# The triangular blocks of an RWKV-7 layer turned by VectorE and merged on chip

## The chip, the cores and the metric

The kernel runs as one launch on one core of a Trainium2 chip. The metric is the device time of that launch in microseconds (us); less is better. TensorE is called PE, VectorE DVE, ScalarE ACT, GpSimd POOL and SyncE SP, as in the profile. SP does nothing but issue DMAs, in order; each other engine also works through its own queue in order.

## What is computed

Two layers of a decoder trunk over 1024 positions of width 1024, in float32. The first layer mixes tokens with RWKV-7, the second with a sparse attention; each is followed by a SwiGLU feed-forward and a layer norm, and every part is scaled and shifted by a vector made from the conditioning `c`. The change lies in the RWKV-7 mixer alone:

```python
def _rwkv7_step(S, inp):
    r_t, w_t, k_t, v_t, a_t, b_t = inp
    sa = jnp.einsum('bhij,bhj->bhi', S, a_t)
    S = S * w_t[:, :, None, :] + sa[..., None] * b_t[:, :, None, :] + v_t[..., None] * k_t[:, :, None, :]
    y = jnp.einsum('bhij,bhj->bhi', S, r_t)
    return S, y
...
xs = h[None] + xx[None] * mu[:, None, None, :]
r, k, v = jnp.einsum('pbtd,pde->pbte', xs[:3], w_rkv)
w = -jax.nn.softplus(-(w0 + jnp.tanh(xw @ w1) @ w2)) - 0.5
a = jax.nn.sigmoid(a0 + (xa @ a1) @ a2)
...
_, y = lax.scan(_rwkv7_step, S0, (tm(rh), tm(decay), tm(kh), tm(vh), tm(-kk), tm(kk * ah)))
```

The kernel does not walk through 1024 steps. It takes 16 chunks of 64 positions; inside a chunk the product of the steps becomes the inverse of a triangular 64x64 matrix for each of the 16 heads. Chunk and head make a *unit*: 256 units, 128 in each half of the sequence.

## The kernel before

Everything is kept feature-major: a tile has 128 partitions (two heads of 64 features: a *feature tile*, `ft`, 8 of them) and 512 positions (a half, `hf`, with 8 chunks). Matmuls of the projections are done as three float32r products of a high and a low part (`mm3`, lines 234 to 236).

**Order in time.** A scheduler lays the program onto the engines when it is built, from dependences, the written order and its own durations; what it decides is fixed, and `order` listings below show it. By the trace the first 976 us go like this. Half 0: the head (modulated and transposed input, `rwkv_head`), then in `rwkv_proj` the low-rank parts (L497), the k projection with `k_rest` for each feature tile (to 204 us), the v projection (to 272), the r projection (to 363), into whose end the head of half 1 is interleaved (L385 on DVE makes the mixed inputs, L437 to L440 on PE multiply them). Half 1: L497 from 380, k to 510, v to 568, r to 625. Then the *core*, `chain_chunk` and `pre_chunk`, which goes through the 16 chunks from 625 to 976 (L954 is the first product of a chunk, L989, L1003, L1016, L1019 its chain), with the output projection of finished quarters (`tail`, L1070) between. The feed-forward and the second layer follow.

**The triangular blocks.** `k_rest` makes on PE the 64x64 products of each unit (L572) and masks them on DVE into `en` (L574), which goes to DRAM as `nsd` (L575). A unit's inverse is made from two 32x32 diagonal blocks and one block below. `tinv_dve` inverts diagonal blocks of 128 units at once, one unit per partition, so a block of rows has to become a row per unit: eight POOL DMAs gather it from `nsd` (L627). One *pass* over 128 blocks is 31 steps of two DVE operations (L634, L636; here called T), and there are two passes for each half. The result is turned by one copy (L641) and goes back to DRAM by POOL (`t1d` L639, `tsd` L642). `tinv_merge` makes the block below for 32 units at a time: POOL loads (L651 to L653), 32x32 products on PE (L659), copies on ACT (L660), again, and a store by POOL (L663). Merges of half 0 lie in the v and r loops of half 1, those of half 1 in the core's chunks 1 to 4. `load_chunk` (L933) loads a chunk's inverses into `ttp` by four DMAs on SP.

**Queues around it.** Spilled r, k, v, a, b and the bonus go out on SP (L519, L521, L617), the weights come in on SP (L215). Tiles named `tmp` are a ring of 7 that ACT, DVE and SP's stores share. The low half of a weight (L122) is made on DVE or POOL in turn.

Of the kernel before, what the change touches and what calls it, by code (L numbers as in the profile page):

```python
# [19 lines left out]
P = 128  # L20
# [23 lines left out]
C_ID, C_CEN, C_M, C_M64, C_RST, C_CS, C_CN, C_BLK, C_E4 = 0, 128, 256, 512, 576, 640, 768, 896, 1024  # L44
C_ALL = 1025


def constants():
# [10 lines left out]
    a[:, C_RST:C_RST + 64] = (t != 0)[None, :]  # L59
    a[:, C_CS:C_CS + P] = np.where(p[None, :] <= p[:, None], 0.0, LOWEST)  # L60
    a[:, C_CN:C_CN + P] = np.where(p[None, :] <= p[:, None], 0.0, NEG)
# [20 lines left out]
def trunk(ctx, tc, a, out):  # L82
# [30 lines left out]
    dma2 = nc.gpsimd.dma_start  # L113
# [28 lines left out]
    csr = cp.tile([P, 8, 32], F32, name="csr")  # L142
# [8 lines left out]
    V.tensor_copy(csr, pt[:, 0:8, None].to_broadcast([P, 8, 32]))  # L151
# [33 lines left out]
    ones = cp.tile([P, 1], F32, name="ones")  # L185
    V.memset(ones, 1.0)
    mhalf = cp.tile([P, 8], F32, name="mhalf")
    V.memset(mhalf, -0.5)
    gne = cp.tile([P, 1], F32, name="gne")
# [61 lines left out]
    def ada_mm(o, st, k0):  # L251
        for i, s_ in enumerate(st):
            k = k0 + i
            q = 32 * (k % 4)
            mm(o[q:q + 32, :], csr[:, k, :], s_, start=k < 4, stop=k >= 4, skip_group_check=True)
# [40 lines left out]
    def ada_v(l, j, stage, tmp):  # L296

        acc = tmp()
        for k2 in range(4):
# [3 lines left out]
            for i in range(2):  # L303
                k = 2 * k2 + i
                if k == 0:
                    V.tensor_scalar(acc, st[:, 0:512], csr[:, 0, 0:1], None, op0=OP.mult)
                else:
                    V.scalar_tensor_tensor(acc, st[:, i * 512:i * 512 + 512], csr[:, k, 0:1], acc, op0=OP.mult, op1=OP.add)
# [47 lines left out]
    nsd = [tc.dram_tile([KT, P, HN], F32, name=f"nsd{h}") for h in range(2)]  # L356
    tsd = [tc.dram_tile([128, 64, 64], F32, name=f"tsd{h}") for h in range(2)]
    t1d = [tc.dram_tile([128, 32, 32], F32, name=f"t1d{h}") for h in range(2)]
# [96 lines left out]
    def rwkv_proj(hf, p1, head, between, betweenv):  # L455
# [16 lines left out]
        rstb = cst[:, None, C_RST:C_RST + 64].to_broadcast([P, 8, 64])  # L472
        rst = tmp("rst", 1)
        V.tensor_copy(rst.rearrange("p (c t) -> p c t", t=64), rstb)
# [72 lines left out]
        em = []  # L547

        def k_rest(ft, em):
# [17 lines left out]
            en = tmp("en", 2)  # L567
# [6 lines left out]
            V.tensor_tensor(v3(en), v3(o), cst[:, None, C_M64:C_M64 + 64].to_broadcast([P, 8, 64]), op=OP.mult)  # L574
            dma(nsd[hf][ft], en)  # L575
# [45 lines left out]
    def tinv_dve(hf, tp):  # L621

        for b in range(2):
            n_ = tp.tile([P, 32, 32], F32, tag="tn", name="tn")
# [1005 lines left out]
```

## Time and profile before

| | us |
|---|---|
| median of 3 runs | 3288.55 |
| lowest and highest | 3287.1, 3292.51 |
| the profiled execution, its time | 3285.99 |
| the profiled execution, its span in the trace | 3284.2 |

The profile is one execution. Each engine's busy time is a share of the span; PE's granted clock is given as a share of 2.4 GHz (1.00, and 0.50 is 1.2 GHz), so a stretch with 0.75 ran half of its time at each level. In the table by stretches a row has the length, the busy time of each engine with the number of records in brackets, the mean granted clock, the mean busy share of the 16 DMA engines, and the rate in GB/s. PE's busy time over the whole span is 93%, DVE's 66%, ACT's 41%, POOL's 33%; these averages hide that single stretches are limited by other engines.

### The profile page before, as it was taken

The numbers are of one execution on the slowest core, as the hardware profiler recorded it, in microseconds if no ns is written. First come the engines' busy times: TensorE is split into PE (matmuls) and PEld (weight loads), VectorE is DVE, ScalarE is ACT, GpSimd is POOL, SyncE is SP. The second block draws the span as 40 slices with busy tenths as digits, with TensorE's granted clock in tenths as the row PEclk, the third lists the DMA queues.
The fourth block names the chain that finished last, engine by engine and source line by source line (L and its number), as shares of the span: only waits on it lengthen the run. The fifth ranks groups of instructions, "written<-read, shape, count | busy, mean of one in ns | idle before, by whom it ended". The sixth has DMA issues, their size and how long they took to land. (4 is left out here: it accounts for less than half of the span.)

```text
span 3284.2 us, 49028 instructions
## 1 busy us (share of the span) xinstructions
PE 3047.2 (93%) x17857; PEld 2401.8 (73%) x17857; DVE 2167.8 (66%) x4255; ACT 1350.7 (41%) x2510; POOL 1090.6 (33%) x946
## 2 busy tenths in 40 slices
PE   6988899889999999999899999988999999899998
PEld 2555367678877788888688776677887777687886
DVE  4577888646776665494245487886697788775345
ACT  3552463234444222332223756656522566452223
POOL 3363257442123411251113213555222432443111
PEclk8989999889999999999999999989999999999999
DMA  6466365788854665382534432153323421353333
GB/s 197 134 188 169 89 195 132 160 164 184 188 140 137 200 196 170 116 269 91 116 103 128 138 96 65 58 163 120 98 92 107 137 64 34 100 164 97 93 100 122
DMA packets 540997, 436.34 MB, mean 133 GB/s; under 512 B 134802, under 2 KB 435346, under 8 KB 540754
## 3 DMA queue, kind: packets, MB, share of 16 engines
q1 hardware_dynamic: 534770, 423.74, 44.9%
q0 software_dynamic: 5984, 9.45, 1.5%
q8 instruction: 141, 2.31, 0.3%
q14 instruction: 102, 0.84, 0.1%
HBM read 378.07 MB, written 54.90 MB: 132 GB/s over the span
## 5 line engine op out<-in xcount | busy, mean ns | idle before, releaser
L205 ACT CAST whi<-wst 128x512 fp32r<-128x512 f32 x886 | 541.0, 619 | 1231.8 <-PE psu L235 541.6
L122 POOL TENSOR_TENSOR wlo<-wst,whi 128x512 fp32r<-128x512 f32 x330 | 460.0, 1394 | 1425.6 <-ACT whi L205 1372.1
L122 DVE TENSOR_TENSOR wlo<-wst,whi 128x512 fp32r<-128x512 f32 (+1 forms) x556 | 472.8, 853 | 518.0 <-ACT whi L205 512.7
L234 PE MATMUL psu<-hin,whi 128*128 128x512 f32 (+1 forms) x1568 | 586.8, 375 | 46.0 <-DVE sl L1168 29.7
L235 PE MATMUL psu<-hin,whi 128*128 128x512 f32 (+1 forms) x1568 | 585.6, 373 | 9.7 <-DVE hin L901 3.3
L236 PE MATMUL psu<-hin,wlo 128*128 128x512 f32 (+1 forms) x1568 | 583.5, 372 | 0.1
L234 PEld LDWEIGHTS psu<-hin,whi 128*128 128x128 f32 x1568 | 300.6, 192 | 101.5 <-DVE sl L1168 33.1
L235 PEld LDWEIGHTS psu<-hin,whi 128*128 128x128 f32 x1568 | 301.6, 192 | 61.4 <-DVE hin L901 6.1
L236 PEld LDWEIGHTS psu<-hin,wlo 128*128 128x128 f32 x1568 | 301.1, 192 | 50.5 <-POOL wlo L122 0.5
L235 PE MATMUL psg<-wlo,hid 128*128 128x512 f32 x528 | 206.4, 391 | 0.0
L234 PE MATMUL psg<-whi,hid 128*128 128x512 f32 x528 | 205.1, 391 | 0.0
L236 PE MATMUL psg<-whi,hid 128*128 128x512 f32 x528 | 205.0, 389 | 0.0
L234 PE MATMUL psg<-xs,whi 128*128 128x512 f32 x384 | 159.2, 425 | 22.5 <-ACT whi L205 11.8
L235 PE MATMUL psg<-xs,whi 128*128 128x512 f32 x384 | 162.2, 422 | 9.6 <-POOL xs L122 5.0
L236 PE MATMUL psg<-xs,wlo 128*128 128x512 f32 x384 | 159.3, 417 | 3.2 <-DVE wlo L122 3.2
L1168 DVE TENSOR_TENSOR sl<-sl,psu 128x512 f32<-128x512 f32 (+1 forms) x98 | 61.8, 630 | 138.0 <-PE psu L236 132.2
L234 PEld LDWEIGHTS psg<-xs,whi 128*128 128x128 f32 x384 | 75.1, 197 | 55.6 <-ACT whi L205 14.6
L234 PEld LDWEIGHTS psg<-whi,hid 128*128 128x128 f32 x528 | 99.2, 188 | 20.9
L236 PEld LDWEIGHTS psg<-whi,hid 128*128 128x128 f32 x528 | 99.1, 188 | 20.8
L235 PEld LDWEIGHTS psg<-wlo,hid 128*128 128x128 f32 x528 | 99.2, 188 | 20.7 <-DVE wlo L122 0.4
L116 ACT ACTIVATE z<-z,mx 128x128 f32<-128x128 f32 (+7 forms) x128 | 99.2, 776 | 31.9 <-DVE mx L1533 31.1
L235 PEld LDWEIGHTS psg<-xs,whi 128*128 128x128 f32 x384 | 75.4, 196 | 41.4 <-POOL xs L122 10.2
(424 smaller groups left out, 6562.3 us busy)
## 6 DMA issues: line engine op xcount, KB each, us to landing
wst<-in_ffn_w_in_dram SPq DMA_DIRECT2D x196, 512.0 KB
wst<-in_ffn_w_out_dram SPq DMA_DIRECT2D x92, 512.0 KB
z<-in_ada_w_dram SPq DMA_DIRECT2D x56, 512.0 KB
wst<-in_rwkv_w_rkv_dram SPq DMA_DIRECT2D x48, 512.0 KB
wst<-in_rwkv_w_out_dram SPq DMA_DIRECT2D x64, 256.0 KB
wst<-in_dsa_w_out_dram SPq DMA_DIRECT2D x32, 512.0 KB
wst<-in_dsa_w_in_dram SPq DMA_DIRECT2D x26, 512.0 KB
wst<-in_ada_w_dram SPq DMA_DIRECT2D x24, 512.0 KB
```

Source lines behind the costliest of these rows:

```text
L116: return A.activation(o, i, f, **kw)
L122: i = eng.tensor_tensor(lo, x, hi.bitcast(F32), op=OP.subtract)
L205: A.copy(h_[:, :m], st[:, c:c + m])
L234: mm(o, lh, rh, start=first, stop=False)
L235: mm(o, lh, rl, start=False, stop=False)
L236: mm(o, ll, rh, start=False, stop=last)
L1168: V.tensor_tensor(sl[:, c], sl[:, c], ou[:, c], op=OP.mult)
```

## The change

The triangular blocks no longer go through DRAM between `k_rest` and the inverse. `k_rest` masks its product into two tiles for every four feature tiles (`nm0`, `nm1`: the columns 0 to 31 and 32 to 63 of each unit; two DVE operations 128x256 in place of one 128x512). After the fourth feature tile a new generator `tinv` is queued: DVE's 32x32 block transposes bring the blocks from rows to units (one of 128x1024 and two of 32x1024), the 31 steps follow as before (they read the turned block in contiguous runs), two more transposes turn the result back, and the merge's products are made straight from these tiles (`nm0`, `xt`, `t1`) with 32 units to a copy. A pass now holds both diagonal blocks of the 64 units of four feature tiles, where it held one block of 128 units. `invert(n)` takes n steps of the passes that are queued: 4 after each feature tile of the v loop, 9 in the r loop, the rest at the end of the half's own `rwkv_proj`. The results go to DRAM on SP as `tdd` and `tod`, and `load_chunk` loads them with six DMAs of 128-byte runs in place of four of 128 and 256 bytes. No DMA of this part is on POOL any more (166 were). Smaller edits: the conditioning `csr` is kept once and broadcast by the matmul's operand, the constants are 833 columns in place of 1025, `rst` is set by memsets, one mask is made from another.

```diff
-        ti = [tinv_dve(hf, tpA) for hf in range(2)]
+        def invert(n):
+            for _ in range(n):
+                while inv and next(inv[0], inv) is inv:
+                    inv.pop(0)
...
         def between0(i):
...
                 take(hg[1], 1)
+                invert(9)
+            if i == 16:
+                invert(100)
...
-        rwkv_proj(0, p1, heads[0], between0, lambda i: take(ti[0], 0))
+        rwkv_proj(0, p1, heads[0], between0, lambda i: invert(4))
...
-            V.tensor_tensor(v3(en), v3(o), cst[:, None, C_M64:C_M64 + 64].to_broadcast([P, 8, 64]), op=OP.mult)
-            dma(nsd[hf][ft], en)
+            for i in range(2):
+                c_ = slice(32 * i, 32 * i + 32)
+                V.tensor_tensor(nm_[i][:, ft % 4], v3(o)[:, :, c_],
+                                cst[:, None, C_M64 + 32 * i:C_M64 + 32 * i + 32].to_broadcast([P, 8, 32]), op=OP.mult)
+            if ft % 4 == 3:
+                inv.append(tinv(hf, ft // 4, *nm_))
...
+        turn = lambda o, i: V.transpose(o, i)
+        turn(n_, fl(n0).rearrange("p u t -> p t u"))
+        for q in (1, 3):
+            turn(n_[qs[q]], fl(n1)[qs[q]].rearrange("p u t -> p t u"))
...
+        xt = tpA.tile([P, 32, 32], F32, tag="tn", name="xt")
+        turn(xt.rearrange("p u t -> p t u"), x_)
+        t1 = tpA.tile([P, 32, 32], F32, tag="tx", name="t1")
+        turn(t1, xt)
+        dma(tdd[hf][:, 4 * g:4 * g + 4].rearrange("p a c t -> p (a c t)"), xt.rearrange("p u t -> p (u t)"))
+        yield
+        for i in range(2):
+            us = range(16 * i, 16 * i + 16)
+            rhs = xt[:, 16 * i:16 * i + 16]
+            for lh, ro in ((fl(n0), 1), (t1, 0)):
+                o = pst()
+                for e in range(2):
+                    k, m = qs[2 * e + ro], qs[2 * e]
+                    for u in us:
+                        v = u - 16 * i
+                        mm(o[m, v * 32:v * 32 + 32], lh[k, u, :], rhs[k, v, :], start=True, stop=True)
+                r_ = inv_tmp[0]()
+                for e in range(2):
+                    A.copy(r_[qs[2 * e]], o[qs[2 * e], :])
+                rhs = r_.rearrange("p (u t) -> p u t", t=32)
+            for e in range(2):
+                dma(tod[hf][e, :, 4 * g + 2 * i:4 * g + 2 * i + 2].rearrange("r a c t -> r (a c t)"), r_[qs[2 * e]])
+            yield
...
             for e in range(2):
-                for r, j in ((0, 0), (32, 32)):
-                    last = dma(tt_[64 * e + r:64 * e + r + 32, :, e, j:],
-                               dap(tsd[hf], (c * 16 + e) * 4096 + r * 64 + j, [[64, 32], [2 * 4096, KT], [1, 64 - j]]))
+                r0 = 64 * e
+                dma(tt_[r0:r0 + 32, :, e, 0:32], tdd[hf][r0:r0 + 32, :, c, :])
+                dma(tt_[r0 + 32:r0 + 64, :, e, 32:64], tdd[hf][r0 + 32:r0 + 64, :, c, :])
+                last = dma(tt_[r0:r0 + 32, :, e, 32:64], tod[hf][e, :, :, c, :])
...
-            if 1 <= gc < 5:
-                tinv_merge(1, gc - 1, pc)
```

Where the work stands on the engines follows from the new written order. Three places matter below. In the listings `tt` and `tx` are the tiles of the inverse's steps, `psg` a projection's PSUM bank, `xs` the mixed input; lines of before and after differ by a few (L381 after is L385 before, L663 after is L659 before, L643 and L645 are the steps L634 and L636).

**First place: DVE at the end of half 0's k loop.** Before, this stretch holds only the work of `k_rest`, the mixing of the v inputs (L385, L126) and low halves of weights; the steps begin some 30 rows further down.

```order
L552 COPY f_111<-d 128x8
L558 TENSOR_TENSOR tmp<-tmp,av 128x512
L385 SCALAR_TENSOR_TENSOR tmp<-h,vf,tmp 128x512
L122 TENSOR_TENSOR xs<-tmp,xs 128x512
L126 TENSOR_SCALAR xs<-tmp 128x512
L574 TENSOR_TENSOR en<-pst,cst 128x512
```

After, the three transposes (L629) that turn the first four feature tiles and the first steps of pass 1 stand among the same work:

```order
L554 TENSOR_TENSOR tmp<-tmp,av 128x512
L629 STREAM_TRANSPOSE tn<-nm_982 128x1024
L119 TENSOR_TENSOR wlo<-wst,whi 128x512
L556 TENSOR_TENSOR sp<-tmp,em 128x512
L629 STREAM_TRANSPOSE tn<-nm_983 32x1024 x2
L552 SCALAR_TENSOR_TENSOR sp<-tmp,d 128x512
L643 TENSOR_TENSOR tt<-tn,tx 128x31
L587 TENSOR_SCALAR tmp<-psu 128x512
```

Pass 1 moved forward into the k loop's end; in half 1 the same happens with pass 3 (rows of the same kind).

**Second place: the seam between half 0 and half 1.** On PE before, the r projection's end (L234 to L236) is interleaved with the head of half 1:

```order
L235 MATMUL psg<-xs,whi 128x512
L236 MATMUL psg<-xs,wlo 128x512
L439 MATMUL psl<-tmp,lr 128x512
L440 MATMUL pst<-tmp,lr_2000 32x512
L437 MATMUL psl<-tmp,lr 64x512
L438 MATMUL psl<-tmp,lr 64x512
L439 MATMUL psl<-tmp,lr 128x512
L440 MATMUL pst<-tmp,lr_2000 32x512
L614 MATMUL psu<-tmp,cst 128x512
```

After, the 128 merge products of pass 2 stand in a row ahead of all of that head (L433 after is L437 before):

```order
L231 MATMUL psg<-xs,whi 128x512
L232 MATMUL psg<-xs,wlo 128x512
L663 MATMUL pst<-xt,nm_1370 32x32 x32
L663 MATMUL pst<-tmp,t_2571 32x32 x32
L663 MATMUL pst<-xt,nm_1370 32x32 x32
L663 MATMUL pst<-tmp,t_2571 32x32 x32
L615 MATMUL psu<-tmp,cst 128x512
L230 MATMUL psg<-xs,whi 128x512
```

On DVE at the same seam the steps of pass 2 were strung out between the head's mixing and half 1's decay (L509, a scan):

```order
L634 TENSOR_TENSOR tt<-tn,tx 128x256
L385 SCALAR_TENSOR_TENSOR sp<-h,vf,sp 128x512
L122 TENSOR_TENSOR xs<-ta,xs 128x512
L126 TENSOR_SCALAR xs<-sp 128x512
L636 TENSOR_TENSOR tx<-tx,tt 128x16x16
L509 SCALAR_TENSOR_TENSOR tmp<-rst,tmp 128x512
L126 TENSOR_SCALAR xs<-sp 128x512
L634 TENSOR_TENSOR tt<-tn,tx 128x255
```

After, all of pass 2 and its two transposes come before the last 18 of the head's mixing operations:

```order
L645 TENSOR_TENSOR tx<-tx,tt 128x2x30
L643 TENSOR_TENSOR tt<-tn,tx 128x31
L645 TENSOR_TENSOR tx<-tx,tt 128x31
L629 STREAM_TRANSPOSE xt<-tx 128x32x32
L629 STREAM_TRANSPOSE t_2571<-xt 128x1024
L636 MEMSET tx 128x1024
L613 SCALAR_TENSOR_TENSOR tmp<-psg,vf,kt 128x512
L637 MEMSET tx 128x32
L381 SCALAR_TENSOR_TENSOR tmp<-h,vf,tmp 128x512 x4
```

**Third place: PE at the start of the core.** Before, half 1's merges are strung between the products of the chunks, here of chunk 2 and 3:

```order
L954 MATMUL psg<-ctar_5150,ctbk_5149 128x2x64 x4
L659 MATMUL pst<-m_5600,m_5598 32x32 x8
L954 MATMUL psg<-ctar_5150,ctbk_5149 128x2x64 x4
L1016 MATMUL psg<-S,ctar_5150 64x64
L659 MATMUL pst<-m_5600,m_5598 32x32 x8
L659 MATMUL pst<-mr,m_5599 32x32 x8
L1016 MATMUL psg<-S,ctar_5150 64x64 x9
L659 MATMUL pst<-mr,m_5599 32x32 x8
```

After, the last 128 of them stand ahead of the core's first product, and the core has none:

```order
L232 MATMUL psg<-xs,wlo 128x512
L663 MATMUL pst<-xt,nm_3819 32x32 x32
L663 MATMUL pst<-tmp,t_4932 32x32 x32
L663 MATMUL pst<-xt,nm_3819 32x32 x32
L663 MATMUL pst<-tmp,t_4932 32x32 x32
L313 MATMUL pst<-cst,modf 40x128
L615 MATMUL psu<-tmp,cst 128x512 x3
L965 MATMUL psg<-ctar_4748,ctbk_4747 128x2x64 x8
```

From chunk 7 of the core on, PE's order is the same in both kernels.

## Rows read from the trace of the kernel before

**Rows 1.** The page's first part: busy time, share and instructions of each engine
```profile
PE 3047.2 (93%) x17857; PEld 2401.8 (73%) x17857; DVE 2167.8 (66%) x4255; ACT 1350.7 (41%) x2510; POOL 1090.6 (33%) x946
```
**Rows 2.** Busy time by stretches: length, PE, PEld, DVE, ACT, POOL, clock, DMA share, GB/s
```profile
200.00:235.00 35.00, 26.27 (x188) 19.77 (x186) 35.00 (x48) 15.11 (x25) 24.53 (x16) 0.90 0.46 132
...
318.00:360.00 42.00, 28.12 (x64) 10.33 (x64) 22.84 (x46) 12.86 (x20) 4.55 (x5) 0.80 0.41 110
360.00:410.00 50.00, 43.09 (x126) 21.11 (x125) 46.73 (x74) 25.04 (x39) 15.22 (x11) 0.93 0.32 76
...
470.00:510.00 40.00, 30.92 (x201) 23.23 (x201) 40.00 (x51) 15.89 (x25) 27.77 (x18) 0.81 0.47 136
...
568.00:625.00 57.00, 49.66 (x345) 34.67 (x343) 27.72 (x59) 8.39 (x19) 32.21 (x45) 0.94 0.62 164
625.00:660.00 35.00, 30.88 (x454) 28.01 (x456) 31.45 (x83) 10.19 (x17) 8.58 (x13) 0.86 0.98 156
660.00:707.00 47.00, 35.85 (x531) 32.24 (x526) 19.82 (x46) 15.06 (x31) 15.10 (x26) 0.75 0.95 192
707.00:765.00 58.00, 56.51 (x1034) 49.99 (x1034) 36.61 (x85) 26.74 (x61) 28.88 (x49) 1.00 0.72 139
```
**Rows 3.** Groups by line, 100 to 980: line, engine, tiles, count, busy us, mean ns, idle
```profile
L636 DVE TENSOR_TENSOR tx<-tx,tt 128x31 f32<-128x31 f32 (+15 forms) x124 | 51.1, 412 | 2.9
L634 DVE TENSOR_TENSOR tt<-tn,tx 128x31 f32<-128x31 f32 (+15 forms) x124 | 49.7, 401 | 8.6 <-DMA m<-nsd 6.0
...
L960 DVE TENSOR_TENSOR g<-psg,cst 128x256 f32<-128x256 f32 x64 | 26.0, 406 | 0.0
...
L627 POOL DMA_DIRECT2D tn<-nsd x32 | 20.0, 632 | 4.3 <-DMA tsd<-tn 3.6 <-issue 0.8
...
L509 DVE TENSOR_TENSOR_SCAN tmp<-rst,tmp 128x512 f32<-128x512 f32 x15 | 19.3, 1286 | 1.2 <-ACT tmp L116 1.2
...
L978 ACT COPY uv<-pst 64x512 f32<-64x512 f32 x32 | 18.6, 580 | 10.4 <-PE pst L974 9.9
...
L574 DVE TENSOR_TENSOR en<-pst,cst 128x512 f32<-128x512 f32 x16 | 10.9, 679 | 0.0
...
L641 DVE COPY tn<-tx 128x1024 f32<-128x1024 f32 x4 | 4.3, 1080 | 0.1
```
**Rows 4.** PE's waits, 318 to 360: engine, tile, line, releaser, us, times, longest
```profile
PE psl L437 <- DVE tmp L385: 9.0, 1, 9.0
PE psl L439 <- DVE tmp L385: 4.9, 1, 4.9
```
**Rows 5.** ACT's longest waits, 300 to 345
```profile
ACT tmp L116 <- DMA bod<-tmp: 29.2, 2, 18.4
```
**Rows 6.** DVE's busy time by stretch in line 636 alone
```profile
380.00:425.00 45.00, 6.35 (x17) 0.92 0.43 112
```
**Rows 7.** DVE's busy time by stretch in line 634 alone
```profile
380.00:425.00 45.00, 5.43 (x16) 0.92 0.43 112
```
**Rows 8.** PE's waits, 568 to 625
```profile
PE psu L614 <- DVE tmp L612: 4.0, 3, 2.6
PE psu L614 <- DVE tmp L615: 2.7, 1, 2.7
```
**Rows 9.** PE and PEld by stretches in line 659 alone, the merges' products
```profile
660.00:707.00 47.00, 8.11 (x144) 7.11 (x144) 0.75 0.95 192
707.00:765.00 58.00, 14.40 (x368) 12.39 (x368) 1.00 0.72 139
```
**Rows 10.** PE's longest wait, 660 to 707
```profile
PE pso L1070 <- DVE whi L122: 6.5, 1, 6.5
```
**Rows 11.** DMA queues, 625 to 707: packets, MB, share of 16 engines
```profile
q1 hardware_dynamic: 32551, 13.14, 86.9%
q0 software_dynamic: 839, 1.24, 8.6%
```

More of the change, by code (lines that the diff above doesn't have):

```diff
@@ L141, in trunk @@
     banks(sa, "psA", t=2,u=1,g=3,l=2)
-    csr = cp.tile([P, 8, 32], F32, name="csr")
+    csr = cp.tile([P, 8], F32, name="csr")
     st0 = wp.tile([P, 1024], F32, tag="wst", bufs=3, name="wst")
@@ L184, in trunk @@
     omka = cp.tile([P, 8], F32, name="omka")
[L185 removed]
+    kc = cp.tile([P, 10], F32, name="kc")
+    mhalf, ones, gne = kc[:, 0:8], kc[:, 8:9], kc[:, 9:10]
+    V.memset(mhalf, -0.5)
     V.memset(ones, 1.0)
[L187 to L189 removed]
     V.memset(gne, GN_EPS)
@@ L355, in trunk @@
     vad = [tc.dram_tile([P, 3, KT, HN], F32, name=f"var{h}") for h in range(2)]
-    nsd = [tc.dram_tile([KT, P, HN], F32, name=f"nsd{h}") for h in range(2)]
-    tsd = [tc.dram_tile([128, 64, 64], F32, name=f"tsd{h}") for h in range(2)]
-    t1d = [tc.dram_tile([128, 32, 32], F32, name=f"t1d{h}") for h in range(2)]
+    tdd = [tc.dram_tile([P, KT, 8, 32], F32, name=f"tdd{h}") for h in range(2)]
+    tod = [tc.dram_tile([2, 32, KT, 8, 32], F32, name=f"tod{h}") for h in range(2)]
     sgd = [tc.dram_tile([160, HN], F32, name=f"sgd{h}") for h in range(2)]
@@ L471, in rwkv_proj @@
         dd, av, sig = [], [], [None]
-        rstb = cst[:, None, C_RST:C_RST + 64].to_broadcast([P, 8, 64])
-        rst = tmp("rst", 1)
-        V.tensor_copy(rst.rearrange("p (c t) -> p c t", t=64), rstb)
+        rst = p1.tile([P, HN], BF16, tag="rst", bufs=1, name="rst")
+        V.memset(rst, 1.0)
+        V.memset(rst[:, 0:HN:64], 0.0)
         def low_rank_in():
@@ L566, in k_rest @@
             spill("k", k2)
-            en = tmp("en", 2)
+            if ft % 4 == 0:
+                nm_[:] = [tpA.tile([P, 4, 8, 32], F32, tag=f"a{i}", bufs=2 - i, name=f"nm{i}") for i in range(2)]
             o = pst()
@@ L645, in tinv_merge @@
[L645 to L663 removed]
+    inv = []
@@ L665, in trunk @@
+    inv_tmp = [None]
     sc0 = ExitStack()
@@ L712, in between1 @@
             if i < 8:
-                take(ti[0], 9)
                 take(ad, 1)
@@ L717, in between1 @@
                     g2_order()
-                if i > 8:
-                    take(ti[1], 9)
+                invert(9)
                 if i == 15:
@@ L724, in between1 @@
             else:
-                take(ti[1])
+                invert(100)
         n1, vl = [0], vec_loads()
```

81 lines of the change are left out of this document (26 added, 55 removed).

## The prediction

> **What bounds the kernel now.** I read the shares first: PE 93%, DVE 66%, ACT 41%, POOL 33% [rows 1]. PE is the bound on average, so time is lost where PE idles or runs at a lower clock, and work added elsewhere costs only where it makes PE idle. Next I read the stretches between 200 and 765 us, the only part that the change touches: before it nothing but small setup moves, and from chunk 7 of the core PE's order is the same. In each row of [rows 2] the reader is to compare PE's busy time with the length, then ask which other engine is full. Two stretches have DVE busy for their whole length, 35.00 of 35.00 (200 to 235) and 40.00 of 40.00 (470 to 510), while PE is busy 26.27 and 30.92: at the seam from the k to the v projection of each half DVE is the bound, and each us of DVE work added there is a us of the kernel. Between 318 and 360 both idle (PE 28.12 and DVE 22.84 of 42): PE waits 9.0 and 4.9 us for the mixed inputs of half 1 [rows 4], these wait for ACT, and ACT for `tmp` tiles whose bonus stores have not gone out, 29.2 us in two waits [rows 5]. From 660 to 707 PE is busy 35.85 of 47 at a clock of 0.75 and the DMA engines 0.95.
>
> **The change, part by part.** Durations are those of the profiled execution (3285.99 us; span 3284.2); it lies 2.56 below the median, and I carry a difference found in the trace over to the median unchanged.
>
> Prices first. A T step stays as it was: 124 + 124 operations, 51.1 + 49.7 us [rows 3], some 25 us for each of the four passes. A transpose has no row. The nearest is L641, which turns the same 128x1024 elements by a strided copy: 1080 ns. Below that I see no reason to go, since as many elements are read and written; above, the slowest row per element on DVE is the scan L509, 1286 ns for 512 columns, so 2572 for 1024. I take 1080, the row with the same job. That the two 32x1024 pieces cost as much as a full one follows from the same count of elements per partition. Five transposes a pass are 5.4 us, where L641 was 1.1. The mask: two 128x256 operations at the 406 ns of L960 for one of 679 (L574), 0.13 more for each feature tile, 1.1 for each half. The 166 POOL issues (L627 shows 632 ns each; 134 more on five lines) vanish, but POOL is not waited for much where they stand; taken at nothing, at best it helps the low halves of weights. ACT's copies become half as many at 580 ns (L978) and stay on an engine with idle time.
>
> A, k to v in half 0: the mask (1.1), the three transposes that turn pass 1 (3.2), and some ten of its first, short steps (0.3 each, 3) come into a stretch in which DVE has no idle time. *+7*; by the scan's price +11.5, and +4 if the steps slip behind the mixing.
>
> On the price there is a rule to weigh. The Trainium skill, "VectorE: DVE Perf Modes", section "The three transpose paths", gives 311 ns for a 128x128 transpose in bf16 on VectorE. As an estimate from that page eight of those are 2.5 us for 128x1024, close to the scan's bound and not to the copy's row; no run here shows it. By that figure A would be +11.
>
> B, the seam between the halves. All of pass 2 now stands on DVE ahead of the last mixing of half 1's head, and on PE 128 merge products ahead of the head's. Before, 33 of the 62 steps came after 380, beside the k stage: 6.35 + 5.43 = 11.8 us [rows 6, 7], about 9.4 net since neighbours overlap by a fifth. So DVE has 9.4 + 5.4 us more to do before L497. Part goes into the 19 us that DVE idles from 318 to 360, waiting for ACT: the transposes and the first twenty steps stand ahead of the blocked mixing, and free some 6 us behind it. The rest, 9 us, is late. The merges take 10 us of PE (14.40 us for 368 records [rows 9], each product being two records: 256 records) plus two rounds of copies at 580 ns in which nothing else can run; most of it goes while DVE does the last 18 mixings, 2 us do not. *+11*. At worst nothing is absorbed and the merges are in series: +25. At best all fits into the idle 19: 0. On SP `tdd` and `tod` now wait for this pass with the weights of half 1's k projection queued behind them (L215); these are needed only after L497, and cost nothing unless the pass is later than that.
>
> C, the k stage of half 1 loses those 33 steps: DVE was busy 46.73 of 50 there [rows 2]. *-9* (-12 to -5).
>
> D, k to v in half 1: as A, with the stretch just as full. *+8* (+4 to +12.5).
>
> E, v and r of half 1. Half 0's merges leave and half 1's come in at about the same 20 us. Pass 4 must finish before the core's first product, and its 128 merges, 10 us, stand alone; against that go the 6.7 us for which PE waits here for L612 and L615 [rows 8], because DVE, busy 27.72 of 57, loses pass 4's tail to the stretch ahead. *+2* (-5 to +12).
>
> F, the start of the core. The merges leave: 8.11 + 14.40 = 22.5 us of PE [rows 9], and in 625 to 660 DVE (31.45 of 35) is rid of the rest of pass 4. What stays is the wait of 6.5 us for the gate's weights [rows 10], which are loaded and converted first; the idle time that merges filled opens again, the idle time of their own waits closes. *-22*. At least the stretch that PE fills (707 to 765) gains, with half of its 14.4 lost to new waits: -8. At most 16.8 us of idle and some 16 of low clock in 625 to 765 shrink by half as well: -38.
>
> Loads of the core: 1536 runs of 128 bytes for each chunk in place of 1024. At 625 to 707 a packet of SP's queue takes 0.869 x 82 x 16 / 32551 = 0.035 us of an engine, so 512 more are 1.1 us of the sixteen for each chunk; POOL's queue, 8.6% or 7 us of that stretch, is gone [rows 11]. Even, so zero.
>
> The sum: 7 + 11 - 9 + 8 + 2 - 22 = **-3**, a profiled execution of 3283 and a median of 3285.5.
>
> **The rivals.**
>
> 1. *Faster by some 24 (3264.5).* The steps of pass 2 fill DVE's blocked time (B = 0) and pass 4 is done when the r projection ends (E = -5), the core gives 25: 7 + 0 - 9 + 8 - 5 - 25 = -24. For it: DVE idles 19 of 42 at the seam and half of 568 to 625. Against: steps and merges are a chain, and the mixing stands behind them.
>
> 2. *Slower by some 21 (3309.5).* The two inversions become waits in front of PE: pass 2's last transpose comes after the r projection of half 0 has run out, PE stands with 128 products and the whole head behind them; and the same with pass 4 before the core: 7 + 25 - 9 + 8 + 12 - 22 = +21. It decides from the point where the last transpose is more than some 13 us later than the last r product, since about that much wait is in the trace already (9.0 + 4.9). For it: PE's new order has nothing left to do there but a bonus product and two or three of the projection.
>
> 3. *The core does not give (3299.5).* PE's idle time from 625 to 707 is not the merges' doing but that of transfers (DMA 0.95 to 0.98) and of the chain from chunk to chunk; the merges ran in its gaps and their leaving gains 8: -3 + 14 = +11. Against: from 707 to 765 PE is full, with 14.4 us of merges.
>
> 4. *Transposes at the scan's pace.* Each 1.5 us dearer: three in A and D (+9), five in pass 2 at half (+4): -3 + 13 = +10, 3298.5. The page on VectorE above has about this price, the row of L641 speaks against it.
>
> **How the numbers follow.** Forecast 0.40, rival 1 0.25, rival 2 0.17, rival 3 0.12, rival 4 0.06. The forecast's own range by the bounds of its terms, taken as independent, is some 20 either way, most of it from B and F. A difference of 0.2% is 6.6 us, about what a measurement of this kernel can tell from no change. Of the forecast's 0.40 I count 0.12 as faster than that, 0.25 within, 0.03 slower. With rival 1 faster is 0.37; with 0.03 of rivals 3 and 4, within is 0.28; slower is 0.35. The range 3263 to 3309 reaches to rivals 1 and 2 and leaves out about half of each, 2 in 10. Likeliest: 3285.5.
>
> **What would show it.** In the profile after: transposes of 128x1024 near 1.08 us (a price near 2.5 is rival 4). DVE full again at both k-to-v seams, these longer by 6 to 9 us. L497 of half 1 starting near 398 in place of 380 (near 388 is rival 1, beyond 410 rival 2), with PE's longest wait in front of L663. The k stage of half 1 shorter by 9. The core's first product (L965 after) near 645 in place of 626, and its stretch up to chunk 7 shorter by 22 (by under 10 is rival 3). Wrong altogether would be a new wait that no term has: SP held by `tdd` or `tod` so long that weights or chunk loads come late, or ACT short of `tmp` tiles since the merges take some.

## The result, and the profile after

The changed kernel took 3329.03 us (median of 4 runs, 3328.73 to 3334.55) beside 3287.82 for the kernel before on the same chip: a ratio of 1.0133, interval [1.0117, 1.0149]. It is 41 us slower, where 3 us faster was forecast, and lies 20 us above the range. The profiled execution of it took 3334.55 us (span 3332.6), 5.5 above its median. In the changed kernel line numbers differ a little: the steps are L643 and L645, the transposes L629, the merges' products L663 and their copies L666, the head's mixing L381 with its products L433 to L436, and L493 is L497 of before, L965 the core's first product (L954 before), L1000 a chunk's chain (L989 before).

The page's first line, answering [rows 1], shows that it is not a matter of work: PE is busy 3050.5 us in place of 3047.2, DVE 28 more.

```profile
PE 3050.5 (92%) x17857; PEld 2417.1 (73%) x17857; DVE 2196.3 (66%) x4289; ACT 1346.9 (40%) x2478; POOL 993.0 (30%) x780
```

Where the time went is read from four starts, and the end of PE's work, in the two traces (us from the span's start):

| | before | after | difference |
|---|---|---|---|
| first product of the r projection of half 0 | 272.4 | 275.0 | +2.6 |
| first L497 (L493) of half 1 | 380.4 | 421.8 | +41.4 |
| first product of the core | 625.7 | 684.4 | +58.7 |
| first L989 (L1000) of chunk 7 | 797.5 | 833.2 | +35.7 |
| PE's last product | 3269.6 | 3317.8 | +48.2 |

So the seam between the halves lost 39 us and what lies between L493 and the core 17: 2 in the k stage, 2 in the v projection, 13 in the r projection of half 1 and its end. The core gave 23 back. The busy times by stretches of the changed kernel, with columns as in [rows 2]:

```profile
200.00:235.00 35.00, 27.22 (x143) 20.34 (x141) 30.98 (x56) 11.59 (x19) 27.07 (x15) 0.83 0.26 70
318.00:375.00 57.00, 26.27 (x88) 14.57 (x88) 39.14 (x76) 11.97 (x19) 8.04 (x6) 0.77 0.26 83
375.00:392.00 17.00, 13.23 (x255) 12.83 (x253) 0.96 (x1) 3.46 (x6) 0.00 (x0) 0.50 0.17 56
392.00:422.00 30.00, 26.69 (x69) 8.16 (x66) 18.11 (x28) 16.79 (x25) 0.00 (x0) 0.87 0.22 57
...
609.00:684.00 75.00, 64.78 (x610) 50.01 (x608) 47.73 (x95) 12.41 (x21) 10.30 (x12) 0.81 0.32 96
684.00:833.00 149.00, 131.17 (x1848) 115.61 (x1848) 92.97 (x212) 55.61 (x103) 22.05 (x29) 0.91 0.85 161
```

The third row is to be looked at: from 375 to 392 DVE is busy 0.96 us of 17, ACT 3.46, POOL not at all, and PE runs at 0.50, its lower level. Three timelines of this place show why (start, us, engine, line, tiles, count, and in brackets the idle time before it with its releaser). PE:

```profile
374.74 3.43 PE L663 MATMUL pst<-xt,nm 32*32 32x32 f32 x64 [20.66 <-DVE xt L629]
379.43 3.43 PE L663 MATMUL pst<-tmp,t 32*32 32x32 f32 x64 [1.25 <-ACT tmp L666]
384.12 3.43 PE L663 MATMUL pst<-xt,nm 32*32 32x32 f32 x64 [1.26 <-ACT tmp L666]
388.80 3.43 PE L663 MATMUL pst<-tmp,t 32*32 32x32 f32 x64 [1.25 <-ACT tmp L666]
394.02 2.08 PE L615 MATMUL psu<-tmp,cst 128*128 128x512 f32 x2 [1.79 <-DVE tmp L613]
```

PE waits 20.66 us for `xt`, the first of the two transposes that turn pass 2's result back, then does the four groups of 32 products (64 records each) one after the other. The second to the fourth wait 1.25 us each for the copies of the group ahead. All run at the low clock that follows the idle time: 3.43 us a group, where a group of pass 1, with the clock at 1.00, took 2.11:

```profile
278.01 2.11 PE L663 MATMUL pst<-xt,nm 32*32 32x32 f32 x64
```

Not all of half 1's head stands behind the merges, as the listing of the second place has it: a quarter (16 of its 64 records of L433 to L436) stands ahead of them, and there PE waits 10.1 us for the mixing, at 341 us. ACT:

```profile
378.21 1.16 ACT L666 COPY tmp<-pst 32x512 f32<-32x512 f32 x2 [9.94 <-PE pst L663]
382.89 1.18 ACT L666 COPY tmp<-pst 32x512 f32<-32x512 f32 x2 [3.52 <-PE pst L663]
387.58 1.16 ACT L666 COPY tmp<-pst 32x512 f32<-32x512 f32 x2 [3.52 <-PE pst L663]
392.26 1.18 ACT L666 COPY tmp<-pst 32x512 f32<-32x512 f32 x2 [3.52 <-PE pst L663]
393.46 3.17 ACT L113 ACTIVATE tmp<-h,ommu 128x512 f32<-128x512 f32 x5
```

ACT's queue holds the copies ahead of the inputs for the head's mixing (L113), so it makes none of these until the merges are over. DVE:

```profile
372.78 1.91 DVE L629 STREAM_TRANSPOSE xt<-tx 128x1024 f32<-128x1024 f32 x1
374.72 1.25 DVE L629 STREAM_TRANSPOSE t<-xt 128x1024 f32<-128x1024 f32 x1
392.51 0.91 DVE L636 MEMSET tx<- 128x1024 f32 x1 [16.54 <-PE pst L663]
393.34 0.63 DVE L613 SCALAR_TENSOR_TENSOR tmp<-psg,vf,kt 128x512 f32<-128x512 f32 x1
...
394.22 2.74 DVE L381 SCALAR_TENSOR_TENSOR tmp<-h,vf,tmp 128x512 f32<-128x512 f32 x4 [0.18 <-ACT tmp L113]
```

DVE's next instruction is the memset that prepares the tile of pass 3, the very row shown in the listing ahead of the prediction. That tile (`tx`) has one buffer, in which the second transposed result (`t`) lies that the merges still read, so DVE stands 16.54 us, with the last 18 mixings behind it. The merges are thus in the queues of PE, ACT and DVE at once, and nothing else goes on.

Why pass 2 ends so late is seen further up on DVE:

```profile
289.65 6.15 DVE L629 STREAM_TRANSPOSE tn<-nm 128x1024 f32<-128x1024 f32 x3 [3.41 <-PE pst L663]
298.76 0.91 DVE L636 MEMSET tx<- 128x1024 f32 x1 [2.24 <-PE pst L663]
...
329.55 0.38 DVE L645 TENSOR_TENSOR tx<-tx,tt 128x207 f32<-128x207 f32 x1
340.87 0.75 DVE L381 SCALAR_TENSOR_TENSOR tmp<-h,vf,tmp 128x512 f32<-128x512 f32 x1 [10.94 <-ACT tmp L113]
342.13 0.86 DVE L643 TENSOR_TENSOR tt<-tn,tx 128x220 f32<-128x220 f32 x1
```

Its own transposes and its memset wait for pass 1's merges, which read the same tiles. Then 18 of its 62 step operations are done when DVE comes to a mixing that has no input yet; DVE stands 10.94 us, and the other 44 operations stand behind that mixing.

### The profile page after: what moved, and what is told of

The parts are those of the page before. It is cut to its first block, busy times and chain, and to the rows that moved or that the text cites. A ratio compares the mean times of both kernels' runs of the same rounds, so it can differ in the third digit from the quotient of the medians.

```text
span 3332.6 us, 48733 instructions
## 1 busy us (share of the span) xinstructions
PE 3050.5 (92%) x17857; PEld 2417.1 (73%) x17857; DVE 2196.3 (66%) x4289; ACT 1346.9 (40%) x2478; POOL 993.0 (30%) x780
## 5 line engine op out<-in xcount | busy, mean ns | idle before, releaser
L113 ACT ACTIVATE z<-z,mx 128x128 f32<-128x128 f32 (+7 forms) x128 | 99.2, 776 | 32.5 <-DVE mx L1542 31.6
```

Source lines behind the costliest of these rows:

```text
L113: return A.activation(o, i, f, **kw)
```

## The experiments

All ratios are to the kernel before on the same chip. L493 (L497), core and chunk 7 are the starts named above, from the profiled execution of each; the last column is the core from its first product to chunk 7. Two things limit what the table shows. The starts are of one execution: before, e4, e7 and e12 have the same order on PE up to the core, and their cores start between 620.9 and 626.7. And an edit changes dependences, so the scheduler may lay other work differently too; in e2 the order on PE, DVE, ACT and POOL is that of the changed kernel, in the other edits of the changed kernel it is not quite.

| run | ratio, interval | L493 | core | chunk 7 | core to chunk 7 |
|---|---|---|---|---|---|
| before | | 380.4 | 625.7 | 797.5 | 171.8 |
| after | 1.0133 [1.0117, 1.0149] | 421.8 | 684.4 | 833.2 | 148.8 |
| e1_memset_pool | 1.0085 [1.0069, 1.0100] | 411.5 | 670.9 | 819.4 | 148.5 |
| e2_flat_turns | 1.0130 [1.0115, 1.0145] | 421.3 | 679.0 | 827.3 | 148.3 |
| e3_pass2_late | 1.0095 [1.0078, 1.0112] | 384.3 | 676.3 | 822.7 | 146.4 |
| e4_before_six_loads | 0.9994 [0.9984, 1.0003] | 379.8 | 620.9 | 788.7 | 167.8 |
| e5_merges_late | 1.0080 [1.0063, 1.0097] | 377.7 | 673.7 | 821.4 | 147.7 |
| e6_eight_steps | 0.9983 [0.9971, 0.9994] | 396.3 | 636.1 | 785.2 | 149.1 |
| e7_before_no_merges_half1 | 0.9902 [0.9886, 0.9918] | 379.2 | 624.1 | 766.7 | 142.6 |
| e8_merges_late_pool | 1.0082 [1.0065, 1.0098] | 378.3 | 669.4 | 818.3 | 148.9 |
| e9_no_merges | 0.9906 [0.9889, 0.9924] | 381.1 | 613.2 | 761.3 | 148.1 |
| e10_products_on_pool | 1.0184 [1.0167, 1.0201] | 431.8 | 699.8 | 848.7 | 148.9 |
| e11_pass2_late_pool | 1.0069 [1.0044, 1.0093] | 384.6 | 668.9 | 816.2 | 147.3 |
| e12_before_merges_one_chunk_later | 1.0004 [0.9993, 1.0015] | 382.0 | 626.7 | 805.7 | 179.0 |
| e13_merges_spread | 1.0143 [1.0127, 1.0160] | 415.7 | 690.8 | 836.5 | 145.7 |
| e14_merges_spread_slow | 1.0043 [1.0026, 1.0060] | 386.1 | 658.7 | 805.9 | 147.2 |
| e15_merges_unchained | 0.9972 [0.9962, 0.9981] | 390.2 | 635.5 | 785.4 | 149.9 |
| e16_merges_spread_fast_half1 | 1.0086 [1.0069, 1.0103] | 382.7 | 675.2 | 825.0 | 149.8 |

### What the parts cost: four runs that take one away

**Merges left out (e9).**

```diff
-            for lh, ro in ((fl(n0), 1), (t1, 0)):
-                o = pst()
...
-                    A.copy(r_[qs[2 * e]], o[qs[2 * e], :])
-                rhs = r_.rearrange("p (u t) -> p u t", t=32)
+            r_ = t1[:, 16 * i:16 * i + 16].rearrange("p u t -> p (u t)")
```

> The changed kernel without the merges: their 512 products and the copies on ACT are left out, and the stores take another tile of the same size; steps and transposes stay. Theory (steps and transposes on DVE hold up what comes before the core; the merges' 42 us of PE lie in waits that would be there anyway): 10 to 20 us faster than the changed kernel. Rival (the merges in a row, in which PE, ACT and DVE wait for each other, are the cost): 35 us or more faster.

It took 3256.23 us, 73 less than the changed kernel. My theory, that steps and transposes on DVE were the cost, fell: with all of them in place L493 starts at 381.1, as in the kernel before. DVE has 80.2 us of work at the seam, in 102 us (the first row below), and it costs nothing there. Pass 2 even ends about as late as in the changed kernel, `xt` at 373.1 (second row) beside 374.7; nothing on PE stands behind it.

```profile
275.00:377.00 102.00, 84.47 (x277) 43.42 (x276) 80.20 (x151) 32.89 (x58) 13.19 (x10) 0.93 0.44 133
...
371.13 1.97 DVE L629 STREAM_TRANSPOSE xt<-tx 128x1024 f32<-128x1024 f32 x1
```

**Merges kept, chain cut (e15).** The products take the masked tiles as operands, so none waits for a pass's steps, and DVE's memset does not wait for them. The second group of each pair still waits for the copies of the first.

```diff
-            rhs = xt[:, 16 * i:16 * i + 16]
-            for lh, ro in ((fl(n0), 1), (t1, 0)):
+            rhs, rq = fl(n0)[:, 16 * i:16 * i + 16], 1
+            for lh, ro in ((fl(n0), 1), (fl(n0), 0)):
```

> The changed kernel with all its merges, but their operands are the masked tiles in place of the transposed results, so that no product waits for a pass's steps; the number of products, copies and DMAs is the same, and the written place too (the output is then another). Theory (of the 73 us that leaving the merges out gave, the products' own time is some 42 and the waiting for the chain the rest): 25 to 35 us faster than the changed kernel, near 3300. Rival (all of it is work and low clock): within 10 us of the changed kernel.

3279.36 us: 50 less than the changed kernel, below the kernel before, and more than the theory asked for. Against e9, which keeps the stores, the products and copies cost 23 us here, about half of the 44 us that PE is busy with the products in the changed kernel. What released L663 after idle time in the changed kernel (PE and the weight load counted apart, which doubles the wait of 20.7):

```profile
  DVE xt L629: 51.3, 4
  issue: 12.5, 7
  ACT tmp L666: 10.9, 10
```

and in e15:

```profile
  issue: 9.3, 16
  ACT tmp L666: 3.2, 2
  PE psg L231: 0.4, 1
```

So 50 of the 73 us go when merges and passes no longer wait for each other. This is the main finding. It takes in more than PE's wait: pass 2's steps begin at 280 in place of 301, as its transposes no longer wait for pass 1's merges, and the scheduler lays pass 2's products, which need nothing of the pass, in pieces among the others from 331 on:

```profile
331.39 0.50 PE L663 MATMUL pst<-nm 32*32 32x32 f32 x10
338.07 2.90 PE L663 MATMUL pst<-nm 32*32 32x32 f32 x54
349.12 2.11 PE L663 MATMUL pst<-tmp,nm 32*32 32x32 f32 x64
```

How the 50 us divide between PE's waits, the tiles held by the merges and this order, the run does not tell.

**Eight steps of 31 (e6).**

```diff
+            if s >= 8:
+                yield
+                continue
             V.tensor_tensor(tv, n_[:, s, s + 1:32, None]...
```

> The changed kernel with 8 of the 31 steps of each pass; 184 of 248 DVE operations are left out, some 74 us of DVE, while transposes, merges, copies and DMAs stay. Theory (DVE's load ahead of the core is the cost, since passes that lay beside the k stage and the core of the kernel before now lie in stretches where DVE is full): the seams close, the core keeps its 23 us, and the time is 3265 to 3280, below the kernel before. Rival (PE's merges, with their copies and the low clock after each wait, are the cost): 3305 or more.

3282.87 us, 46 less than the changed kernel, a little above what the theory gave. By itself it seemed to show DVE's load as the cost; e9 shows that the same load is free when nothing waits for its end. What the run shortened was the chain. L493 still starts 16 us late.

**The kernel before without half 1's merges (e7).**

```diff
-            if 1 <= gc < 5:
-                tinv_merge(1, gc - 1, pc)
...
-                               dap(tsd[hf], (c * 16 + e) * 4096 + r * 64 + j, ...
+                               dap(tsd[0 if r == 0 else hf], (c * 16 + e) * 4096 + r * 64 + j, ...
```

> The kernel before without the merges of half 1 in the core: neither their products nor copies nor POOL's DMAs; the core loads half 0's blocks in their place. Theory (the merges were what the changed kernel's core gained by leaving): core from its first product to chunk 7 shorter by 18 to 25 us, the kernel by as much (3267). Rival (the steps of pass 4, which lie in 625 to 656 of the kernel before, were it): under 10 us.

3258.04 us, 32 less than before; the core to chunk 7 is 29 shorter. The products had 22.5 us [rows 9]. The rest is seen in the stretch from 660 to 707, where [rows 2] had a clock of 0.75:

```profile
624.00:660.00 36.00, 33.49 (x534) 30.41 (x534) 32.52 (x87) 12.57 (x21) 6.32 (x9) 0.91 0.95 160
660.00:707.00 47.00, 37.38 (x571) 32.53 (x572) 26.33 (x62) 15.32 (x29) 5.12 (x7) 0.93 0.96 193
707.00:767.00 60.00, 59.52 (x757) 51.12 (x757) 46.57 (x105) 28.80 (x55) 12.45 (x15) 1.00 0.85 170
```

It is 0.93 here. The DMA engines are as full as before (0.96), and PE still idles 9.6 us of these 47 (11.2 before): that idle time was not the merges' doing, as rival 3 had it, but the gain is 29 and not its 8. The steps of pass 4 still lie at the core's start, so these were not the gain either.

### Prices in dispute

**Contiguous transposes (e2).**

```diff
-        turn(n_, fl(n0).rearrange("p u t -> p t u"))
+        turn(n_, fl(n0))
...
-        turn(xt.rearrange("p u t -> p u t"), x_)
+        turn(xt, x_)
```

> The changed kernel, with every transpose reading and writing contiguous rows; the inverse is then of the wrong arrangement, and the order on every engine is the same. In the changed kernel a strided one takes 1.9 to 2.0 us, a contiguous one 1.245. Theory (their price is the smaller part): each pass loses four times 0.7 us, of which pass 2 and pass 4 feel it, and the k-to-v seams two thirds: 5 to 8 us faster than the changed kernel (3322). Rival (the price of the transposes is the cause): 15 us or more faster.

No gain: 3331.27 us. Here are the transposes of the changed kernel (ns: shortest, median, longest), and below them those of this run:

```profile
L629 DVE STREAM_TRANSPOSE tn<-nm x12: 1925/2000/2132, 184.7 to 618.7; 32x1024 f32<-32x1024 f32 x8, 128x1024 f32<-128x1024 f32 x4
L629 DVE STREAM_TRANSPOSE xt<-tx x4: 1904/1918/1965, 268.2 to 659.2; 128x1024 f32<-128x1024 f32 x4
L629 DVE STREAM_TRANSPOSE t<-xt x4: 1231/1245/1245, 271.5 to 661.1; 128x1024 f32<-128x1024 f32 x4
```

```profile
L629 DVE STREAM_TRANSPOSE tn<-nm x12: 1234/1238/1245, 185.0 to 611.5; 32x1024 f32<-32x1024 f32 x8, 128x1024 f32<-128x1024 f32 x4
L629 DVE STREAM_TRANSPOSE xt<-tx x4: 1230/1245/1246, 268.9 to 654.5; 128x1024 f32<-128x1024 f32 x4
```

Sixteen of the twenty fell by 0.7 us. The core starts 5 us earlier, no more than single starts scatter, and chunk 7 to the end is as much longer in that execution; by the ratios the price of the transposes is not the cause. My 5 to 8 us were too much, and rival 4 is nearer the price of the strided ones than I was and wrong on the effect.

**Six loads in the kernel before (e4).**

```diff
-                for r, j in ((0, 0), (32, 32)):
+                for r, j in ((0, 0), (0, 32), (32, 32)):
```

> The kernel before, with a chunk's inverses loaded by six DMAs of 128-byte runs in place of four. Theory (the loads are hidden, and what the changed kernel loses after chunk 7 is something else): within 2 us of the kernel before. Rival (more and shorter runs slow the core, where the DMA engines are near full): 5 us or more slower, in the chunks.

3286.83 us, ratio 0.9994 with an interval of some 3 us to either side: the shorter runs of the chunk loads cost nothing that shows.

**The steps' products on POOL (e10).**

```diff
-            V.tensor_tensor(tv, n_[:, s, s + 1:32, None]...
+            G.tensor_tensor(tv, n_[:, s, s + 1:32, None]...
```

> The changed kernel with the first of the two operations of each step (L643, 124 of them, 49 us) on POOL, which is idle at the seam: DVE has 40 us less to do before the core, the chain of a pass becomes longer, since POOL is slower and each step changes engine twice. If DVE's load is the cost: 15 us or more faster than the changed kernel. If the length of the chain is the cost (PE waits for its end): 10 us or more slower.

3346.99 us, 18 slower than the changed kernel. The products that left DVE took it 55 us, and its busy time falls by 33, but a step now takes POOL's 596 ns and a change of engine each way:

```profile
L643 POOL TENSOR_TENSOR tt<-tn,tx x124: 237/596/1120, 193.2 to 674.1; 128x31 f32<-128x31 f32 x8, 128x60 f32<-128x60 f32 x8, 128x87 f32<-128x87 f32 x8, 128x112 f32<-128x112 f32 x8
```

Pass 2's `xt` ends at 385.2 in place of 374.7, and L493 starts 10 us later, so the seam moved with the end of the chain; PE's wait in front of the merges did not grow (19.3 us). Less load on DVE and a longer chain is slower, as the theory of the chain has it. What POOL's other work, now behind these products, adds to it the run does not separate. With e9 and e15 the cause is shown: the merges, by their coupling to the passes.

### Moving the waits

**The memsets on POOL (e1).**

```diff
-        V.memset(x_, 0.0)
-        V.memset(x_.rearrange("p a b -> p (a b)")[:, 0:1024:33], 1.0)
+        G.memset(x_, 0.0)
+        G.memset(x_.rearrange("p a b -> p (a b)")[:, 0:1024:33], 1.0)
```

> The changed kernel, but the two memsets that prepare the next pass's tile (L636, L637) are on POOL in place of DVE; the products and their order stay. Theory (DVE stood 16.5 us behind that memset, which waits for pass 2's merges, with the head's mixing queued behind it): the mixing runs beside the merges, L493 of half 1 starts near 406 in place of 421.8, and the kernel is some 15 us faster than the changed one (3314). Rival (the length of the chain of steps, transposes and merges is the cost, and the memset only waits where all wait): L493 at 417 or later, at most 4 us faster.

3317.59 us, 11 less than the changed kernel; L493 at 411.5, between the two expectations. But the mixing does not run beside the merges, as the theory had it. DVE stands all the same, now for ACT's input of the mixing, which is behind the merges' copies in ACT's queue, and PE still waits for the transpose:

```profile
DVE tmp L381 <- ACT tmp L113: 20.5, 6, 17.6
PE pst L663 <- DVE xt L629: 26.0, 1, 26.0
```

So the memset alone was not what held the mixing; ACT's queue holds it as long. What was gained came from the order that the scheduler laid anew: from 318 us on PE waits 1.1 us for the mixing ahead of the merges in place of 10.1, and `xt` is done at 367.3 in place of 374.7.

**Pass 2 in half 1's k stage (e3), and with the memsets on POOL (e11).**

```diff
                 take(hg[1], 1)
-                invert(9)
-            if i == 16:
-                invert(100)
+                invert(1)
...
             if i < 8:
+                invert(7)
                 take(ad, 1)
```

> The changed kernel, but half 0's inversions are taken one step for each feature tile in the r loop and seven for each feature tile of half 1's k loop, so that pass 2 with its merges lies in half 1's k stage. Theory (the seam between the halves is the cost): L493 of half 1 starts near 385 in place of 421.8, the k stage gives back some 10 us, and the kernel is 25 to 30 us faster than the changed one (near 3300). Rival (the DVE work costs the same wherever it lies): under 10 us faster.

> Pass 2 in half 1's k stage, as before in the run with that edit alone, and the memsets on POOL. There DVE's memset waited only 0.8 us, so the wait has nothing more to give: within 4 us of the run with pass 2 late alone (3321). If the memsets' own 4 us of DVE count in full stretches: some 4 us less.

3321.09 and 3311.09 us. The seam is closed in both (L493 at 384.3 and 384.6), but the gain was 8 and not 25 to 30: the 37 us came back by the core's start, which is only 8 and 16 earlier. In e3 the k stage, where DVE is nearly full [rows 2], is 18 longer and the v projection 14, so passes 3 and 4 are pushed against the core. e11 gains some 8 us more than e3, where I gave the memsets at most 4; but the two intervals overlap, so that the difference is not clear.

**Merges 18 turns later (e5), and with the memsets on POOL (e8).**

```diff
         dma(tdd[hf][:, 4 * g:4 * g + 4].rearrange("p a c t -> p (a c t)"), xt...
-        yield
+        for _ in range(18):
+            yield
```

(Half 0's leftover goes to half 1's k loop, at 9 turns.)

> The changed kernel, but each pass waits 18 turns between its last transpose and its merges, and half 0's leftover is taken in half 1's k loop: on PE pass 2's merges now stand behind the whole head of half 1 and the first product of L493, while its steps stay where they were. Theory (the place of the merges is the cost at the seam: PE stands 20.7 us in front of them in order, and DVE 16.5 us behind them): L493 starts near 400 in place of 421.8 and the kernel is 15 to 20 us faster than the changed one (3312). Rival (DVE's work ahead of L493 is the cost, steps and transposes): L493 at 412 or later, under 8 us faster.

> Both edits: merges 18 turns later and the memsets on POOL. If the two causes at the seam are one (DVE and PE standing at the same merges), this gains no more than 4 us over the kernel with late merges alone; if they add, 10 us more.

3315.48 and 3315.74 us. L493 starts at 377.7 and 378.3, earlier than in the kernel before: the merges' place was all of the loss at the seam. But the block took the wait along. In e5, 378 to 460, DVE's longest wait is the same memset behind the same block (L664 in this run):

```profile
DVE tx L636 <- PE pst L664: 20.6, 1, 20.6
```

In e8 the memset is gone from DVE and another instruction waits there, 21.5 us for an input of ACT's, which has the merge's copies ahead of it. The two edits do not add.

**Merges taken apart (e13, e14, e16).** Each of the four groups of a pass is some turns after the one ahead, memsets on POOL; the three differ in the pace.

```diff
             for lh, ro in ((fl(n0), 1), (t1, 0)):
+                for _ in range(8):
+                    yield
                 o = pst()
```

> The changed kernel with all its work, memsets on POOL, and a pass's four groups of 32 products taken 6 turns apart instead of in a row, 9 turns for each feature tile of the v and r loops (6 in half 0's v loop) and 9 in half 1's k loop. Pass 1's groups then lie in the r projection, pass 2's between the products of the head of half 1, pass 4's partly between the last products of r. Theory (the cost is that a pass's merges stand in a row, with PE at the low clock and ACT, DVE and SP waiting): at least 20 us faster than the changed kernel (3308 or less). Rival (merges cost some 70 us wherever they stand, by their work and their chain): less than 15 us faster than the changed kernel, as with the whole block moved.

> As the run before, but slower in half 0 (4 turns for each feature tile in v, 6 in r), with groups 8 turns apart: pass 2 and its merges lie wholly in half 1's k stage between products of the k projection, none at the seam. Theory (merges in a row are the cost): at least 20 us faster than the changed kernel; and since DVE is full in the k stage, slower than the spread at the seam by what the steps cost there, some 5 to 10 us. Rival: as the whole pass 2 moved there, 8 to 18 us faster than the changed kernel, and no more.

> The spread of e14, with half 1 taken at 12 turns for each feature tile in place of 9, so that pass 4's groups stand between products of the r projection instead of ahead of the core. If the last wait ahead of the core is what remains: 5 to 10 us faster than e14 (3301). If DVE's steps are not ready then: as e14 or slower, with PE's waits for xt back.

3333.76, 3301.08 and 3317.24 us. e14 is the best complete version that was found, 28 less than the changed kernel and still 14 above the kernel before; that is what the theory asked for. But pass 2 lies in half 1's k stage here as in e11, and against e11 the gain is 10 us with intervals that overlap. e13, with the groups of pass 2 among the head's products, gave nothing: there PE waited 12.7 us for the mixing and 10.5 ahead of the core. In e16 pass 4's merges were forward in PE's order and its steps not ready:

```profile
PE pst L666 <- DVE xt L629: 15.0, 1, 15.0
```

In e14 the two waits for `xt` are 1.4 and 1.5 us. By these three runs, whether the groups stand in a row or apart matters less than whether the chain is done when PE comes to them; no run changes the one without the other.

**Half 1's merges a chunk later in the kernel before (e12).**

```diff
-            if 1 <= gc < 5:
-                tinv_merge(1, gc - 1, pc)
+            if 2 <= gc < 6:
+                tinv_merge(1, gc - 2, pc)
```

> The kernel before with half 1's merges begun in chunk 2 of the core in place of chunk 1, behind the stretch with the low clock and the full DMA engines. Leaving them out gave 31 us where their products take 22.5, so some 8 us are due to their place: if so, 3 to 8 us faster than the kernel before. If all 31 are their work: within 2 us.

3289.86 us, no difference that shows: of the two expectations the one by which the 31 us follow the merges. The clock was 0.75 from 660 to 707 and 1.00 from 707 to 765 [rows 2]; here it is

```profile
660.00:707.00 47.00, 37.08 (x669) 32.84 (x667) 23.78 (x55) 17.42 (x35) 13.11 (x23) 0.93 0.97 183
707.00:765.00 58.00, 50.23 (x779) 44.80 (x778) 33.55 (x81) 22.41 (x50) 25.25 (x44) 0.85 0.76 139
```

so the low stretch moved on as the merges did. Why the clock is low in just these places no run shows.

## Why the prediction was wrong

**The step that failed is B**, the seam, put at +11 with +25 as its worst; it was +39. Its two largest parts are PE's wait in front of pass 2's merges, 20.7 us, and the merges themselves, 17.5. Three things in B were wrong.

First, the price of the merges. I took 10 us by a row at full clock [rows 9] and two rounds of copies. The products took 13.7 us, since PE ran at 0.50 behind its idle time, and three waits for copies 3.8.

Second, the overlap. I had it that "most of it goes while DVE does the last 18 mixings". DVE did none of them. The memset stood ahead of them in the order that I had listed myself, waiting for the merges' tile; and on ACT their inputs stood behind the merges' copies, which holds them as long when the memset is gone (e1). Of a queue in order, each row between a wait and the work that is counted on has to be asked what it waits for, and so has the queue that feeds that work; I read the steps and the mixing and passed over the rest.

Third, the wait. I counted DVE's work and found 9 us of it late. What PE waits for is not the sum of the work but the end of the chain in DVE's order, and there 44 of the 62 step operations stood behind the blocked mixing; B itself has only some twenty of them ahead of it. DVE still idled 17.9 of the 57 us from 318 to 375, where I had counted on its idle time to take the steps in. The wait for the mixing stayed besides, 10.1 us beside 9.0 and 4.9 before [rows 4].

**E** has the same mistake: +2 was forecast with +12 as its worst, +15 came, 2 in the v projection and 13 in the r projection and its end. Pass 4's merges stand in a row ahead of the core, 14.6 us from 661.2 to 675.9, after a wait of 7.0.

**Rival 2 was the case**, with its mechanism, its two places and its side; it got 0.17. Its condition (more than some 13 us between the last r product and the last transpose) was met by 20.7, and its sign, L493 beyond 410, came. Its price, +21, was half of what came, mostly because its term for the seam was my own bound for B, +25 for the 39.

**A and D** were forecast at +7 and +8 and cost about nothing (A: the r projection starts 2.6 us later) and about 2 with C together. The transposes of pass 1 came at 185 us, ahead of the full stretch, where DVE had idle time (from 165 to 200 it was busy 19.85 us of 35 in the kernel before); from 200 to 235 DVE is busy 30.98 of 35 and no longer full. **C**, -9, is not seen alone: from L493 to the v projection it is 137 us for 135.

**F was right**: -22 forecast, -23.0 measured, and about as much in every variant of the changed kernel (145.7 to 149.9 us for 171.8). e7 shows the mechanism; the same merges gave more there (-29) than their own time, and why the changed kernel's core gained 6 us less stays open. (Half of the 14.4 us is 7.2 and not the 8 that F's lower bound has, which moves rival 3's price by 1.)

**The transposes** took 1.9 to 2.1 us strided and 1.245 contiguous, where I took 1.08 with 2.57 as the bound. The Trainium skill, "VectorE: DVE Perf Modes", "The three transpose paths", from which I had estimated 2.5, is for bf16 blocks of 128x128. By the contiguous row here eight such blocks in float32 cost 1.245 us, half of that estimate; the strided ones lie between the two. e2 shows that the difference moved nothing.

**The unchanged rest**: from chunk 7 to PE's last product took 2472 us before and 2485 after, with nearly the same order on PE. The 18 traces lie between 2472 and 2491 there, and the two profiled executions are 5.5 above and 1.8 below their medians. So these 13 us, a term that the prediction had at nothing, are not clear of the scatter; what moves it stays open.

**The sum as the runs give it**, by medians: without its merges the changed kernel is 32 us below the kernel before; their products and copies, free of the passes, add 23; their coupling to the passes adds 50. The 32 us are not the gain of the rest of the change, since the kernel before has merges too, and no run leaves all of them out of it; half 1's alone are 32 there (e7).

## What to carry to other kernels

Here taking a round trip through DRAM out of a chain also took out its slack: before, the merges' operands were there when PE reached them (in all of the kernel PE idled less than 2 us ahead of their products for another engine, beside 5.9 us of its own issue), and after, the products stood in PE's order right behind the chain that feeds them. When a change moves work forward in a queue that runs in order, ask first when its operands are done, and what on every engine stands behind each of its pieces, the small ones too: a memset for the next round held DVE 16.5 us, and with the memset gone the copies in ACT's queue held it 17.6. Ask then which tiles the moved work holds, since single buffers tie each round to the one ahead. And a busy sum says little on such a block: DVE's work was free where nothing stood behind its end (e9), and PE came back from 20.7 us of idle time at half its clock.

## What the hardware showed that was not expected

- A 32x32 block transpose on DVE of 128x1024 float32 took 1245 ns with contiguous rows and 1904 to 2132 with strides on one side; one of 32 partitions took about as long as one of 128 (medians 1985 and 2079 strided, 1238 and 1240 contiguous). The strided copy of the same size took 1080 [rows 3].
- 64 records of 32x32 products took 3.43 us at a granted clock of 0.50 (1.2 GHz) after 20.7 us of idle time, and 2.11 us at a clock of 1.00.
- An elementwise product of up to 128x256 float32 took POOL 596 ns (median) in a chain with DVE (e10), and DVE 375 in the changed kernel.
